# The opening stage of a decoder trunk: the conditioning vector spread by the matrix engine, low parts of two weights formed there, loads in another order, later work queued behind the stage

## The chip, the cores and the metric

The kernel runs on one core of one Trainium2 chip. The metric is the device time of one execution in microseconds (us). Engines are named as in the profile: PE is TensorE's matmul, PEld its weight load, DVE is VectorE, ACT is ScalarE, POOL is GpSimd, and SP is SyncE, whose queue (SPq) issues nearly all DMAs. The five run side by side, each in the order of its own instruction stream, and wait for each other on semaphores.

## The reference, cut to what matters

One layer of a decoder, sequence 2048, width 1024, float32, batch 1.

```python
c_act = jax.nn.silu(c)                                   # (1, 1024)
mod = (c_act @ w_ada[l] + b_ada[l])[:, None, :]          # 6 * 1024 conditioning values
sh1, sc1, g1, sh2, sc2, g2 = jnp.split(mod, 6, axis=-1)
h = rms_norm(x) * (1.0 + sc1) + sh1
x = x + g1 * token_mixer(h, w_in[l], ...)                # one in-projection, 11 head groups, one out-projection
h = rms_norm(x) * (1.0 + sc2) + sh2
x = x + g2 * conv_ffn(h, w_up[l], ...)
return rms_norm(x) * final_gain
```

Nothing of the in-projection can begin before the norm of the first 512 rows of `x` is known and, for each 128 columns of `h`, the two conditioning values `sc1` and `sh1` of those columns.

## The kernel before

**Tiling.** The 2048 rows are four blocks of 512 (`TB`); the width of 1024 is eight tiles of 128 (`KD`), so a block of `x` is eight tiles x[0] to x[7] of 128 partitions by 512. A product in float32 is made of three products of a rounded type (`F32R`): each operand is split into a high part (a cast) and a low part (the value minus the cast), and `split3` multiplies high by high, high by low and low by high. The high part is an ACT cast; the low part is a DVE subtraction of a 128x1024 tile.

**The opening, `startup()`.** For the first block it does by hand what later blocks find done: eight loads of x[k]; squares on ACT (`sumsq`, L336 and L339) that DVE adds up (L340, tile `san`); a PE product with a column of ones (`ssn`, L412); an inverse square root by Newton steps on DVE (L153 to L158, tile `rsn`); a PE product that spreads it to 512 columns (`bcn`, L420) and an ACT copy of that (`bc`, L423). Then eight steps k. In step k DVE makes x[k] = x[k] * sc1 * bc (`scaled`, L346), ACT makes the high part of `h` (`high`, L350, tile `ha`), DVE its low part (`low`, L353), and PE multiplies the tile by three weight pieces of the first HGRN2 unit: `f` and `q` (L434, into the PSUM tiles `pshfh` and `pshqh`) and `v` (L440, into `psvgh`; `v0` holds the rows of steps 0 to 3, `v1` those of 4 to 7).

**The conditioning.** Each of the 48 groups of 128 values is one DVE instruction over a 128x1024 tile of `w_ada` (`cond` or `ada`, L197, tile `wada`; shown as CUSTOM_DVE_ANT_0 with a short reading of the sum behind it), which multiplies by `c_act`, the activated vector repeated on all 128 partitions. Group 8+k is `sc1` of step k, group k is `sh1`. Sixteen of them lie in the opening. `c_act` is made from `craw`, a load that reads the 4 KB vector once for each partition (L176, 512 KB), a sigmoid on ACT (L177) and a product on DVE (L178).

**Loads.** SP issues them in order. The weights of the opening go into `wraw`, a ring of two buffers (`NRAW`), so the raw piece of `v0` (`rv`) can only be loaded once the low part of `f` has read its buffer. A ring of eight tiles (`a4k`) holds `c_act`, `craw`, the `wada` tiles and the two parts of `v1`.

**What sets the order.** PE's order is written out by hand for the whole kernel (`tc.manual_schedule(engines={PE})`). Inside `startup()` that of DVE, ACT and SP is too. Behind it a scheduler orders DVE, ACT and SP by priority and readiness, and it may place instructions of later code between those of the opening: `gla_weights` (L713 to L719, the small weight `alow`, its DVE row is L717), the weights of the second unit (`rakg`, `raqg`, split at L229 and L233 into `hakg`, `lakg`, `haqg`, `laqg`). The low parts of the weights are stored for later blocks (`keep`, L208).

After the opening PE goes on with `alg` (L728), `psakg`, level products of the first unit (`lvh`, L610) and `psaqg`, without another stage of this kind; the MLP behind it is a long run of `split3` products.

Of the kernel before, what the change touches and what calls it, by code (L numbers as in the profile page):

```python
# [9 lines left out]
F32 = mybir.dt.float32  # L10
# [7 lines left out]
P = 128  # L18
D = 1024
# [81 lines left out]
def trunk(ctx, tc, xT, vecs, cvec, cst, rope, msk, wada, win, walow, wgla, wout, wup, wdown, out):  # L101
# [70 lines left out]


    c_act = pa.tile([P, D], F32, tag="a4k", name="c_act")
    craw = pa.tile([P, D], F32, tag="a4k", name="craw")
    nc.sync.dma_start(craw[:], cvec.to_broadcast([P, D]))  # L176
# [157 lines left out]
    def sumsq(acc, x, k, name, sl=slice(0, TB), first=None, room=None):  # L334
        if k == 0 if first is None else first:
            S.activation(acc[:, sl], x[:, sl], AF.Square)  # L336
        else:
            sq = (room or late)(f"sq{name}{k}")
            S.activation(sq[:, sl], x[:, sl], AF.Square)  # L339
            V.tensor_tensor(acc[:, sl], acc[:, sl], sq[:, sl], op=ALU.add)  # L340
# [4 lines left out]
    def scaled(t, bc, k):  # L345
        V.scalar_tensor_tensor(t, t, SC1[:, k:k + 1], bc, op0=ALU.mult, op1=ALU.mult)  # L346
# [5 lines left out]
    def low(t, k):  # L352
        V.scalar_tensor_tensor(h[k][:, 1, :], t, SH1[:, k:k + 1], h[k][:, 0, :], op0=ALU.add, op1=ALU.subtract)  # L353
# [13 lines left out]
    def new_bc1(b):  # L367
        return px.tile([P, TB], F32, tag="bc1", name=f"bc1_{b}", bufs=1)

    def startup():  # L370
# [5 lines left out]
            nc.sync.dma_start(x[k], xT[0, :, k, :])  # L376
        raws = {}

        def weight(name, i, extra=False):
            raw = pw.tile([P, 1024], F32, tag="wraw", name="r" + name, bufs=NRAW)  # L380
            nc.sync.dma_start(raw[:], win[i])
            if extra:
                t = [pa.tile([P, 1024], F32R, tag="a4k", name=n + name) for n in "hl"]
            else:
                t = [pw.tile([P, 1024], F32R, tag="w" + n, name=n[0] + name) for n in ("hi", "lo")]
            W[name] = [*t, raw, i]

        def cast(name):
            S.copy(W[name][0][:], W[name][2][:])

        def low_part(name):
            hi, lo, raw, i = W[name]
            V.tensor_tensor(lo[:], raw[:], hi[:], op=ALU.subtract)

        def cond(m):
# [18 lines left out]
        V.tensor_scalar(ms[:], ps[:, 0:NCH], 1.0 / D, EPS, op0=ALU.mult, op1=ALU.add)  # L414
        newton(ms, r, NCH)
        cast("f")
        bc = bc1[0] = new_bc1(0)
        ps = late_ps("bcn1_0")
        for c in range(NCH):
            T.matmul(ps[:, c * P:(c + 1) * P], r[:, c:c + 1].to_broadcast([P, P]), ident, start=True, stop=True)  # L420
        cond(0)
        cond(9)
        S.copy(bc[:], ps[:])  # L423
        cast("q")
# [19 lines left out]
        def flush():  # L444
            for q in list(pending):
# [1 line left out]
                    pending.remove(q)  # L447
                    put(*q)

        plan = [((10,), (), (1,), "f"), ((3, 11), (), (2,), "q"), ((4,), (10,), (3,), "v0"),  # L450
                ((12, 5), (11,), (4,), None), ((13, 6), (12,), (5,), "v1"), ((14, 7), (13,), (6,), None),
                ((15,), (14,), (7,), None), ((), (15,), (), None)]
        parts = {"f", "q"}, set()
        for k, (ld, first, then, wl) in enumerate(plan):
            if k == 0:
                weight("v0", 2)
            if k == 3:
                weight("v1", 3, True)
            load(*ld)
            for m in first:  # L460
                cond(m)
            scaled(x[k], bc[:], k)
            high(x[k], k, "0_")
            if k in (1, 4):
                name = "v0" if k == 1 else "v1"
                cast(name)
                parts[0].add(name)
            for m in then:
                cond(m)
            low(x[k], k)  # L470
# [242 lines left out]
    def gla_weights():  # L713
        raw = pt.tile([P, KD, 16], F32, tag="te", name="alraw", bufs=NTE)
        nc.sync.dma_start(raw[:], walow)
        S.copy(alow[:, :, 0:16], raw[:])
        V.tensor_tensor(alow[:, :, 16:32], raw[:], alow[:, :, 0:16], op=ALU.subtract)  # L717
        nc.sync.dma_start(gup[0:16, :], wgla)
        nc.sync.dma_start(gup[16:32, :], wgla)  # L719

    def unit_g(b, pos):
        nm = f"g{b}"
# [315 lines left out]
    jobs = [job for k in range(NF // 2) for job in (("d", k), ("u", 2 * k + 1 if k < 10 else 0))]  # L1038
    for b in range(NB):
        pos = 0  # L1040
        if b == 2:
            later += range(40, 48)
        for i, (kind, u) in enumerate(ORDER):
# [521 lines left out]
```

## Time and profile before

| what | us |
|---|---|
| median of 3 runs | 2544.25 |
| the runs | 2546.16, 2537.70, 2544.25 |
| the profiled execution | 2538.74 |
| its span, first to last instruction | 2537.0 |
| PE busy in the span | 2478.0 (98%) |
| PE busy in the first 59.0 us | 31.97 |
| PE busy from 59.0 to 120.0 us | 61.00 |

Rows of the timeline read: start, length, engine, line, operation, output <- inputs, shape, count, and in brackets how long the engine had been idle and whose end released it. Rows with x above 1 are several instructions in one line. Two DVE instructions that follow each other overlap by about 0.1 us, so the distance of two starts is a little less than a row's length. A list of DMAs gives, for each kind, its size and the median time from issue to landing.

### The profile page before, as it was taken

How to read it: one execution, taken by the hardware profiler on the slowest of the kernel's cores; microseconds unless marked ns; L12 is line 12 of the kernel's file. 1: busy time of each engine (PE TensorE's matmuls, PEld its weight loads, DVE VectorE, ACT ScalarE, POOL GpSimd, SP SyncE). 2: the span in 40 equal slices, each digit the busy share in tenths (PEclk: the TensorE clock that was granted, in tenths of full speed). 3: DMA queues.
4: the chain of work that ended last, by engine and by line, in shares of the span. 5: the costliest groups of instructions: out<-in, count | busy, mean ns of one | idle time of the engine just before them, and what ended most of it. 6: DMA issues, size and time to landing. Idle time of an engine off the chain costs nothing.

```text
span 2537.0 us, 36995 instructions
## 1 busy us (share of the span) xinstructions
PE 2478.0 (98%) x13146; PEld 2106.8 (83%) x13146; DVE 1949.7 (77%) x3568; ACT 1134.1 (45%) x1906; POOL 151.4 (6%) x271
## 2 busy tenths in 40 slices
PE   5999999999999999999999999999999999999998
PEld 4889888888889888898788888888878888888887
DVE  8788985878678676767688888887678777778666
ACT  4433434423443235333455555455445545545442
POOL 1000000000000000000100000000001010010000
PEclk9999999999999999999999999999999999999999
DMA  8454576675687846884754444487665544447653
GB/s 304 163 198 166 197 259 226 223 272 196 221 325 250 286 161 230 294 301 152 236 184 150 161 156 144 145 291 251 203 223 186 159 137 152 151 133 265 215 191 125
DMA packets 228057, 525.45 MB, mean 207 GB/s; under 512 B 24960, under 2 KB 28064, under 8 KB 227872
## 3 DMA queue, kind: packets, MB, share of 16 engines
q1 hardware_dynamic: 224672, 512.60, 59.3%
q0 software_dynamic: 3200, 10.49, 1.2%
q8 instruction: 103, 1.69, 0.3%
q14 instruction: 82, 0.67, 0.1%
HBM read 393.49 MB, written 129.50 MB: 206 GB/s over the span
## 4 chain that ended last, share of the span: by engine, by line
PE 59%; DMA 4%; DVE 4%; issue 1%; ACT 1%; SPq 0%; DVEq 0%; ACTq 0%; POOLq 0%
PE X L241 6%; PE X L242 6%; PE X L243 6%; PE Z L242 3%; PE Z L243 3%; PE Z L241 3%; PE dX L241 3%; PE dX L242 3%; PE dX L243 3%; PE lvh L610 2%; PE Y L242 2%; PE Y L243 2%; PE Y L241 2%; PE psqkvgr L243 1%; PE psqkvgr L241 1%
## 5 line engine op out<-in xcount | busy, mean ns | idle before, releaser
L241 PE MATMUL X<-B,A 128*128 128x512 f32 x572 | 223.1, 390 | 1.4 <-ACT u L1246 1.4
L243 PE MATMUL X<-B,A 128*128 128x512 f32 x572 | 222.6, 389 | 0.0
L242 PE MATMUL X<-B,A 128*128 128x512 f32 x572 | 222.5, 389 | 0.0
L973 DVE TENSOR_TENSOR dA<-rd,dA 128x512 fp32r<-128x512 f32 x154 | 106.3, 691 | 91.2 <-ACT dA L972 90.5
L972 ACT CAST dA<-rd 128x512 fp32r<-128x512 f32 x154 | 95.5, 620 | 148.9 <-PE dX L243 59.6
L242 PE MATMUL dX<-dB,dA 128*128 128x512 f32 x396 | 154.3, 390 | 2.2 <-DVE dB L973 2.2
L241 PE MATMUL dX<-dB,dA 128*128 128x512 f32 x396 | 154.2, 389 | 1.6 <-DVE y L1424 1.6
L243 PE MATMUL dX<-dB,dA 128*128 128x512 f32 x396 | 154.1, 389 | 0.0
L973 DVE TENSOR_TENSOR A<-s,A 128x512 fp32r<-128x512 f32 x176 | 120.8, 687 | 40.5 <-ACT A L972 40.3
L241 PE MATMUL psvgh<-hvgh,ha 128*128 128x256 f32 x480 | 140.9, 293 | 0.0
L243 PE MATMUL psvgh<-hvgh,ha 128*128 128x256 f32 x480 | 136.3, 284 | 0.0
L242 PE MATMUL psvgh<-lvgh,ha 128*128 128x256 f32 x480 | 136.2, 284 | 0.0
L972 ACT CAST A<-s 128x512 fp32r<-128x512 f32 x176 | 108.6, 617 | 56.3 <-PE Z L243 43.5
L241 PEld LDWEIGHTS X<-B,A 128*128 128x128 f32 x572 | 107.5, 188 | 24.4 <-ACT u L1246 2.2
L243 PEld LDWEIGHTS X<-B,A 128*128 128x128 f32 x572 | 107.4, 188 | 22.3
L242 PEld LDWEIGHTS X<-B,A 128*128 128x128 f32 x572 | 107.4, 188 | 22.2
L242 PE MATMUL Z<-B,A 128*128 128x512 f32 x308 | 120.7, 392 | 4.3 <-DVE B L973 4.3
L610 PE MATMUL lvh<-qbh,kh 128*128 128x128 f32 x896 | 120.3, 276 | 1.4 <-DVE nw L157 1.3
L610 PEld LDWEIGHTS lvh<-qbh,kh 128*128 128x128 f32 x896 | 114.7, 190 | 7.8 <-issue 1.8
L241 PE MATMUL Z<-B,A 128*128 128x512 f32 x308 | 120.7, 392 | 0.5 <-ACT B L972 0.5
L243 PE MATMUL Z<-B,A 128*128 128x512 f32 x308 | 120.3, 391 | 0.0
L973 DVE TENSOR_TENSOR dB<-rb,dB 128x512 fp32r<-128x512 f32 x154 | 105.6, 687 | 8.4 <-ACT dB L972 8.3
(458 smaller groups left out, 6981.6 us busy)
## 6 DMA issues: line engine op xcount, KB each, us to landing
gs<-yv SPq DMA_DIRECT2D x154, 256.0 KB, 2.9
rb<-gs SPq DMA_DIRECT2D x154, 256.0 KB, 4.0
r<-wup SPq DMA_DIRECT2D x141, 256.0 KB, 3.3
s<-sumsu SPq DMA_DIRECT2D x132, 256.0 KB, 3.0
wada<-wada SPq DMA_DIRECT2D x48, 512.0 KB, 4.9
rd<-sumsd SPq DMA_DIRECT2D x88, 256.0 KB, 4.0
rd<-wdown SPq DMA_DIRECT2D x66, 256.0 KB, 3.5
x<-xT SPq DMA_DIRECT2D x64, 256.0 KB, 5.7
```

The source lines that it names most:

```text
L241: T.matmul(ps, lhs[0], rhs[0], start=first, stop=False, skip_group_check=more)
L242: T.matmul(ps, lhs[0], rhs[1], start=False, stop=False, skip_group_check=more)
L243: T.matmul(ps, lhs[1], rhs[0], start=False, stop=last, skip_group_check=more)
L610: T.matmul(ps[:, c * P:(c + 1) * P].rearrange("p (h n s) -> p h n s", h=2, s=s), kq[rs, c * P:(c + 1) * P], rhs, start=True, stop=True)
L972: S.copy(hi, src)
L973: V.tensor_tensor(lo, src, hi, op=ALU.subtract)
```

## The change

- `c_act`: the vector is loaded as eight rows of 128 (`c_row`, 4 KB); PE transposes it to a column (`ct`), ACT and DVE activate the 128x8 column (`csig`, `ccol`), eight PE products of 128 columns in float32 spread it over the partitions (`cb`), and ACT copies the two PSUM banks to `c_act`.
- Low parts of `f` and `q`: for each half of 512 columns PE multiplies the raw weight by the identity (float32) and the cast by minus the identity (`minus`, F32R) into one bank, and ACT copies it out (`low_sum`, `low_out`). Those of `v0` and `v1` stay on DVE.
- Loads: `v0` and `v1` get raw buffers of their own (tag `qbd`); the weights and the `wada` tiles of the first steps are issued in another order; the small loads (`alraw`, `gup`, `m_all`) come behind the last `wada` tile.
- `plan`: the conditioning groups of step k+1 are made in step k as before, the order of 2 and 10 is turned; the low part of `v0` comes in step 1 (before: step 2).
- The squares use six buffers in place of two (`room=tmp`).
- `issue_after`: in block 0, everything traced behind `startup()` and `gla_weights()` stands behind three named instructions on SP, ACT and DVE.

```diff
-    craw = pa.tile([P, D], F32, tag="a4k", name="craw")
-    nc.sync.dma_start(craw[:], cvec.to_broadcast([P, D]))
-    S.activation(c_act[:], craw[:], AF.Sigmoid)
-    V.tensor_tensor(c_act[:], c_act[:], craw[:], op=ALU.mult)
+    c_row = pt.tile([KD, P], F32, tag="te", name="c_row", bufs=NTE)
+    nc.sync.dma_start(c_row[:], cvec.rearrange("o (k p) -> (o k) p", p=P))
...
+            if name in "fq":
+                raw = pw.tile([P, 1024], F32, tag="wraw", name="r" + name, bufs=NRAW)
+            else:
+                raw = p1.tile([P, 1024], F32, tag="qbd", name="r" + name, bufs=3)
...
+        def low_sum(name, j):
+            hi, lo, raw, i = W[name]
+            sl = slice(j * 512, (j + 1) * 512)
+            ps = halves[name, j] = lev_ps(f"low{name}{j}")
+            T.matmul(ps[:], ident, raw[:, sl], start=True, stop=False)
+            T.matmul(ps[:], minus[:], hi[:, sl], start=False, stop=True)
+
+        def low_out(name, j):
+            S.copy(W[name][1][:, j * 512:(j + 1) * 512], halves.pop((name, j))[:])
...
-        load(8, 0)
+        load(8)
         weight("f", 1)
-        load(9)
+        load(0)
         weight("q", 0)
-        load(1, 2)
+        load(9, 1)
+        weight("v0", 2)
+        load(10)
+        pc_ = late_ps("ct")
+        T.transpose(pc_[:, 0:KD], c_row[:], ident[0:KD, 0:KD])
+        cs, cc = small("csig", KD), small("ccol", KD)
+        S.activation(cs[:], pc_[:, 0:KD], AF.Sigmoid)
+        V.tensor_tensor(cc[:], pc_[:, 0:KD], cs[:], op=ALU.mult)
+        cb = [lev_ps(f"cb{j}") for j in range(2)]
+        for k in range(KD):
+            T.matmul(cb[k // 4][:, (k % 4) * P:(k % 4 + 1) * P], cc[:, k:k + 1].to_broadcast([P, P]), ident, start=True, stop=True)
...
-            sumsq(acc, x[k], k, "n1_0_")
+            sumsq(acc, x[k], k, "n1_0_", room=tmp)
+        for j in range(2):
+            S.copy(c_act[:, j * 512:(j + 1) * 512], cb[j][:])
+        S.mul(minus[:], ident, -1.0)
         cond(8)
...
-        plan = [((10,), (), (1,), "f"), ((3, 11), (), (2,), "q"), ((4,), (10,), (3,), "v0"),
...
+        plan = [((2,), (1,), (), None, ()), ((11,), (10,), (2,), "v0", ("v0",)), ((3,), (11,), (3,), None, ()),
...
+            scaled(x[k], bc[:], k)
+            high(x[k], k, "0_")
             if k == 0:
-                weight("v0", 2)
...
+                low_sum("f", 1)
+                low_out("f", 1)
+                for j in range(2):
+                    low_sum("q", j)
+                    low_out("q", j)
...
-    nc.sync.dma_start(m_all[:], msk[:, 0:320])
-    gla_weights()
+        last = gla_weights()
+        first = [nc.sync.dma_start(m_all[:], msk[:, 0:320]).ins, *last]
...
+    behind = ExitStack()
+    for ins in first:
+        behind.enter_context(tc.issue_after(ins))
```

Three places of the instruction streams show what moves. The first is DVE's stream in steps 0 and 1 (`x` is `scaled`, `ha` the low part of `h`, ISA the conditioning). Before:

```order
L346 SCALAR_TENSOR_TENSOR x_0_345<-x_0_345,mod,bc_0_419 128x512
L197 ISA wada_371,mod<-wada_371,c_act,vec 128x1024
L197 ISA mod 128x1
L353 SCALAR_TENSOR_TENSOR ha_0_440<-x_0_345,mod,ha_0_440 128x512
L393 TENSOR_TENSOR lf<-rf,hf 128x1024
L346 SCALAR_TENSOR_TENSOR x_0_345<-x_0_345,mod,bc_0_419 128x512
L197 ISA wada_373,mod<-wada_373,c_act,vec 128x1024
L197 ISA mod 128x1
L353 SCALAR_TENSOR_TENSOR ha_1_455<-x_0_345,mod,ha_1_455 128x512
L393 TENSOR_TENSOR lq<-rq,hq 128x1024
L717 TENSOR_TENSOR alow<-alraw,alow 128x8x16
```

The same place of the changed kernel's DVE stream, up to the first row of step 2:

```order
L344 SCALAR_TENSOR_TENSOR x_0_343<-x_0_343,mod,bc_0_444 128x512
L195 ISA wada_369,mod<-wada_369,c_act,vec 128x1024
L195 ISA mod 128x1
L351 SCALAR_TENSOR_TENSOR ha_0_462<-x_0_343,mod,ha_0_462 128x512
L344 SCALAR_TENSOR_TENSOR x_0_343<-x_0_343,mod,bc_0_444 128x512
L195 ISA wada_375,mod<-wada_375,c_act,vec 128x1024
L195 ISA mod 128x1
L351 SCALAR_TENSOR_TENSOR ha_1_491<-x_0_343,mod,ha_1_491 128x512
L195 ISA wada_459,mod<-wada_459,c_act,vec 128x1024
L195 ISA mod 128x1
L394 TENSOR_TENSOR lv_374<-rv_371,hv_373 128x1024
L344 SCALAR_TENSOR_TENSOR x_2_346<-x_2_346,mod,bc_0_444 128x512
```

The rows of `lf`, `lq` and `alow` are gone from here, and that of `lv` for `v0` stands one step earlier.

The second is PE's stream at its beginning, in the changed kernel. Before, the four `ssn` and the four `bcn` products were all that stood ahead of the first `pshfh`.

```order
L422 MATMUL ct<-c_all,c_row 128x8
L428 MATMUL cb_383<-c_all,ccol 128x128 x4
L428 MATMUL cb_384<-c_all,ccol 128x128 x4
L439 MATMUL ssn_0_421<-c_all,san_0_394 128x1 x4
L402 MATMUL lowf_441<-rf,c_all 128x512
L403 MATMUL lowf_441<-hf,minus 128x512
L448 MATMUL bcn_0_445<-c_all,rsn_0_427 128x128 x4
L402 MATMUL lowf_464<-rf,c_all 128x512
L403 MATMUL lowf_464<-hf,minus 128x512
L402 MATMUL lowq_468<-rq,c_all 128x512
L403 MATMUL lowq_468<-hq,minus 128x512
L402 MATMUL lowq_472<-rq,c_all 128x512
```

One half of `f` stands ahead of `bcn`, the other three halves behind it.

The third is SP's queue at the end of the opening. Before, the load of `raqg` stood ahead of the store of `lakg`:

```order
L208 DMA kepti1l<-lf 128x1024
L208 DMA kepti0l<-lq 128x1024
L208 DMA kepti2l<-lv_436 128x1024
L208 DMA kepti3l<-lv_522 128x1024
L228 DMA raqg_784<-win 128x1024
L208 DMA kepti17l<-lakg_732 128x1024
```

In the changed kernel:

```order
L226 DMA rakg_765<-win 128x1024
L206 DMA kepti1l<-lf 128x1024
L206 DMA kepti0l<-lq 128x1024
L206 DMA kepti2l<-lv_374 128x1024
L206 DMA kepti3l<-lv_489 128x1024
L206 DMA kepti17l<-lakg_764 128x1024
L226 DMA raqg_816<-win 128x1024
```

`raqg` now stands behind a store that waits for DVE's low part of the piece before it. From the instructions on that the trace of before shows at about 80 us, the streams of all engines hold the same instructions in the same order in both kernels.

More of the change, by code (lines that the diff above doesn't have):

```diff
@@ L416, in startup @@
         cast("f")
+        low_sum("f", 0)
         bc = bc1[0] = new_bc1(0)
@@ L448, in flush @@
                     put(*q)
-        plan = [((10,), (), (1,), "f"), ((3, 11), (), (2,), "q"), ((4,), (10,), (3,), "v0"),
[L451 to L454, printed above, removed]
-            if k == 0:
-                weight("v0", 2)
-            if k == 3:
-                weight("v1", 3, True)
-            load(*ld)
+        plan = [((2,), (1,), (), None, ()), ((11,), (10,), (2,), "v0", ("v0",)), ((3,), (11,), (3,), None, ()),
+                ((12, 4), (12,), (4,), "v1", ("v1",)), ((13, 5), (13,), (5,), None, ()), ((14, 6), (14,), (6,), None, ()),
+                ((15, 7), (15,), (7,), None, ()), ((), (), (), None, ())]
+        parts = {"f", "q"}, {"f"}
+        for k, (ld, first, then, wl, wc) in enumerate(plan):
+            load(*ld)
+            if k == 1:
+                weight("v1", 3)
+            scaled(x[k], bc[:], k)
+            high(x[k], k, "0_")
+            if k == 0:
+                low_sum("f", 1)
[3 more added lines that the diff above has]
+                    low_out("q", j)
+                parts[1].add("q")
+            for name in wc:
+                cast(name)
+                parts[0].add(name)
             for m in first:
                 cond(m)
[L462 to L467, printed above, removed]
+            low(x[k], k)
             for m in then:
                 cond(m)
-            low(x[k], k)
             if wl:
```

19 lines of the change are left out of this document (12 added, 7 removed).

## The prediction

> **What bounds the kernel now.** First the page and the busy time by stages: PE is the bound, and the opening is the only long stretch where it is not.
>
> ```profile
> span 2537.0 us, 36995 instructions
> PE 2478.0 (98%) x13146; PEld 2106.8 (83%) x13146; DVE 1949.7 (77%) x3568; ACT 1134.1 (45%) x1906; POOL 151.4 (6%) x271
> ...
> 0.00:59.00 59.00, 31.97 (x161) 26.25 (x161) 47.05 (x81) 22.44 (x31) 11.26 (x22) 1.00 0.82 304
> 59.00:120.00 61.00, 61.00 (x338) 49.81 (x339) 43.03 (x94) 30.01 (x56) 1.99 (x3) 1.00 0.52 181
> ```
>
> PE idles 59.0 us in all and 27.0 of them before 59.0 us; in the 61 us behind that it is never idle. So what the opening ends earlier should carry to the end, and nothing else in the kernel changes. The marks of the opening are in PE's and ACT's timelines:
>
> ```profile
> 14.48 1.87 PE L412 MATMUL ssn<-c_all,san 128*128 128x1 f32 x8 [14.48 <-DVE san L340]
> 18.58 2.07 PE L420 MATMUL bcn<-c_all,rsn 128*128 128x128 f32 x8 [2.23 <-DVE rsn L158]
> 30.00 2.08 PE L440 MATMUL psvgh<-hv,ha 128*128 128x256 f32 x8 [3.94 <-ACT hv L389]
> 34.00 1.20 PE L440 MATMUL psvgh<-hv,ha 128*128 128x256 f32 x8
> 55.66 0.50 PE L434 MATMUL pshfh<-ha,hf 128*128 128x512 f32 x1 [0.54 <-DVE ha L353]
> 58.99 0.42 PE L728 MATMUL alg<-ha,alow 128*32 128x512 f32 x1 [0.48 <-ACT snh L691]
> 7.64 0.63 ACT L336 ACTIVATE san<-x 128x512 f32<-128x512 f32 x1 [0.33 <-DMA x<-xT]
> 8.30 2.03 ACT L339 ACTIVATE sqn<-x 128x512 f32<-128x512 f32 x3
> 20.69 0.59 ACT L423 COPY bc<-bcn 128x512 f32<-128x512 f32 x1 [3.52 <-PE bcn L420]
> 16.12 1.04 ACT L389 CAST hf<-rf 128x1024 fp32r<-128x1024 f32 x1 [2.62 <-DMA rf<-win]
> 28.90 1.04 ACT L389 CAST hv<-rv 128x1024 fp32r<-128x1024 f32 x1 [2.42 <-DMA rv<-win]
> 53.85 0.73 ACT L350 ACTIVATE ha<-x,mod 128x512 fp32r<-128x512 f32 x1 [3.14 <-DVE x L346]
> ```
>
> The opening ends at 58.99, where `alg` begins, 3.33 us after the last low part of `h` lets PE go (55.66). That low part is DVE's, so I read DVE's timeline back from there:
>
> ```profile
> 8.96 5.47 DVE L340 TENSOR_TENSOR san<-san,sqn 128x512 f32<-128x512 f32 x7 [0.40 <-ACT sqn L339]
> 21.31 0.75 DVE L346 SCALAR_TENSOR_TENSOR x<-x,mod,bc 128x512 f32<-128x512 f32 x1 [0.37 <-ACT bc L423]
> 23.85 1.22 DVE L393 TENSOR_TENSOR lf<-rf,hf 128x1024 fp32r<-128x1024 f32 x1
> 24.98 0.74 DVE L346 SCALAR_TENSOR_TENSOR x<-x,mod,bc 128x512 f32<-128x512 f32 x1
> 27.51 1.22 DVE L393 TENSOR_TENSOR lq<-rq,hq 128x1024 fp32r<-128x1024 f32 x1
> 28.64 0.28 DVE L717 TENSOR_TENSOR alow<-alraw,alow 128x128 fp32r<-128x128 f32 x1
> 30.16 1.28 DVE L197 CUSTOM_DVE_ANT_0 wada<-wada,c_act,vec 128x1024 f32<-128x1024 f32 x1 [1.23 <-DMA wada<-wada]
> 45.34 0.75 DVE L346 SCALAR_TENSOR_TENSOR x<-x,mod,bc 128x512 f32<-128x512 f32 x1
> 49.20 0.75 DVE L346 SCALAR_TENSOR_TENSOR x<-x,mod,bc 128x512 f32<-128x512 f32 x1
> 53.06 0.75 DVE L346 SCALAR_TENSOR_TENSOR x<-x,mod,bc 128x512 f32<-128x512 f32 x1
> 53.73 1.22 DVE L233 TENSOR_TENSOR lakg<-rakg,hakg 128x1024 fp32r<-128x1024 f32 x1
> 54.86 0.75 DVE L353 SCALAR_TENSOR_TENSOR ha<-x,mod,ha 128x512 fp32r<-128x512 f32 x1
> ```
>
> From 21.31 to 55.61 DVE has one idle row, the 1.23 us for a `wada` load. A step costs 3.86 us (45.34, 49.20, 53.06): a scaling, a low part, two conditionings. PE needs less and waits. So the opening is a front up to 21.31, set by loads and the chain through `san`, `ssn`, `rsn` and `bc`, and then a DVE stretch.
>
> **The change, part by part: the DVE stretch.** The thirteen conditionings, eight scalings and eight low parts of `h` all stay. What leaves:
> - `lf` and `lq`: each takes 1.13 us from its start to the next start (23.85 to 24.98, 27.51 to 28.64). Together -2.26.
> - `alow` and the wait behind it: 28.64 to 30.16, -1.52. The wait goes because SP no longer holds `wada` group 10 behind `rv`, which stood in the queue until `lf` freed a `wraw` buffer; now `rv` has its own.
> - `lakg`: in its place DVE waits for ACT's last high part. From the scaling's start to ACT's start is 0.79, ACT takes 0.73, a hand-over 0.04: 1.56 us, against 1.80 (53.06 to 54.86). -0.24.
> - `lv` for both halves of `v` stays on DVE, one merely a step earlier: 0.
>
> Sum of the stretch: -4.02.
>
> **The front.** DVE's seven adds run without a gap in 5.47 us, 0.78 each, from the end of the second square on. Six buffers for the squares instead of two therefore give nothing; the cover is that DVE chain itself. What counts is when x[1] lands, 8.30 (its square begins ACT's second row). Rows for that:
>
> ```profile
> 1.67 0.42 SPq L176 DMA_DIRECT2D craw<-cvec  x1
> 2.13 4.44 SPq L376 DMA_DIRECT2D x<-xT  x8
> ...
> x<-xT SPq DMA_DIRECT2D x10, 256.0 KB, 5.9
> craw<-cvec SPq DMA_DIRECT2D x1, 512.0 KB, 4.6
> c_all<-cst SPq DMA_DIRECT2D x1, 136.5 KB, 2.6
> ...
> gs<-yv SPq DMA_DIRECT2D x154, 256.0 KB, 2.9
> ```
>
> The 512 KB of `craw` stand just ahead of the eight tiles and become 4 KB. At the rate behind it (tiles of 256 KB landed about 0.65 us apart: the three squares of ACT's second row take 2.03) its bytes alone are worth 1.3 us, so x[1] at 7.0: that end excludes less. The other end: x[1] is issued at about 2.6, and 256 KB with nothing in the way land in 2.9 us, so at 5.5. Between them I take 5.5, since the only large transfer ahead is then x[0] itself, which is nearer to the free transfer than to the queue of before. x[1] comes 2.8 us earlier (bounds 1.3 and 2.8), the last add ends at 11.6, and the chain `ssn`, Newton, `bcn`, `bc` keeps its length of 6.88 us (14.43 to 21.31): -2.8.
>
> What the front adds: the transpose, 8x128 sigmoid and product need `c_row` and the identity in `c_all`, both issued ahead of the x tiles; `c_all` lands 2.6 us after an issue before 1.67, so they are over near 5 us. The eight `cb` products are two `bcn` rows, 4.1 us, on a PE that had no work until 14.48. Two copies to `c_act` (0.59 each, as `bc`) and `minus` follow the last square on ACT, end near 12 and stand ahead only of `hf`, whose raw weight came at 16.12 and now has 1 MB less ahead of it (`craw` and one `wada`), so it comes at 12 to 13 by the same rate. Nothing there is on the path. The later `wada` tiles come one per 1.3 us at that rate, and DVE takes two in 3.86, so none is late. The first half of `f` is made while Newton runs (about 2 us, `bcn` before it started at 14.43 + 4.15).
>
> **The three other halves.** They stand behind `bcn` on PE, and their copies stand on ACT ahead of the second high part, for which DVE waits. A half is 512 columns in float32 and 512 rounded:
>
> ```profile
> 76.51 1.12 PE L739 MATMUL zg<-alg,gup 32*128 32x512 f32 x2
> 24.57 1.05 PE L434 MATMUL pshqh<-ha,hq 128*128 128x512 f32 x2
> ```
>
> At full rate 1.1 us (the `zg` row is one such float32 product with its latency), at the slow rate of the opening 2.1 (the `bcn` row has the same 512 columns; a rounded one costs 0.43). The two `psvgh` rows show the rate: eight products took 2.08 at 30.00 and 1.20 at 34.00, so PE runs at half rate until about 4 us of unbroken work. In the changed kernel unbroken work starts with the first half of `f` at 13.6, so full rate from 17.6, just as `bcn` ends (17.9). The halves end at 19.0, 20.1 and 21.8 (the last needs a bank that is copied out behind ACT's first high part), the copy at 22.4, the second high part at 23.2, and DVE, which would come to the low part at 18.53 + 4.41 = 22.94 (18.53 is where the first scaling now starts; two scalings, a low part, two conditionings), waits 0.3. The bounds: 0, and at the slow rate throughout 2.9. I take +0.3.
>
> The Trainium skill, "TensorE: Matmul & The Clock Gate", Part 1, says that the full rate comes after one busy window of about 3.4 us, that the windows run freely, and that one idle window takes it away. The two `psvgh` rows agree with the first part. By that rule the start at 13.6 could be answered as late as 20.4, an estimate from its two windows, and the sum would be about 0.7 us smaller.
>
> **The sum.** -4.02 - 2.8 + 0.3 = -6.5 us: `alg` at 52.5 in place of 58.99. The profiled execution took 2538.74 (span 2537.0 and 1.7 around it), so 2532.2; it lies 5.5 below the median of the three runs, 2544.25, and the same 6.5 off the median gives the forecast, 2537.7. PE's added work, some 4.1 + 4 halves, is paid out of its 27 idle us.
>
> Later work is cast later: `hakg` and `lakg`, then `raqg`. `lakg` follows the last low part and ends near 51, well before `psakg` would read it (16 `alg` products behind 52.5). `raqg` is the third rival below. The held-back POOL clears of `qbd` buffers now wait for `v0` and `v1`; the first that meets a waiter is used after `psaqg`, 30 us later.
>
> **Rivals.**
> 1. The front moves only by the bytes of `craw` (1.3): the sum is -5.0, 2539.2. For it: the DMA engines are 0.82 busy over the opening, by the row quoted first. Against it: the latency of a free tile.
> 2. PE stays at half rate through the three halves, so DVE waits 2.9: -3.9, 2540.3. For it: PE idles from the `cb` products to `ssn`. Against: the 4 us between the `psvgh` rows.
> 3. Slower than before: `raqg` is late. Its load now waits on SP behind the store of `lakg`, so it is issued near 51.3 (before, at 46.30).
>
> ```profile
> raqg<-win SPq DMA_DIRECT2D x1, 512.0 KB, 6.9
> ...
> 50.00:55.00 5.00, 4.38 (x25) 3.38 (x23) 4.96 (x8) 1.44 (x2) 0.18 (x1) 1.00 0.45 149
> ...
> 69.89 0.48 PE L241 MATMUL psaqg<-ha,haqg 128*128 128x512 f32 x1
> ```
>
>  With 6.9 us to land it is there at 58.2, cast at 59.3 and split at 60.5; `psaqg` wants it at 69.89 - 6.5 = 63.4. So 2.9 us are spare. PE then stops one for one, and the kernel is slower than before only from 9.4 us more on; at 20 us to land it would cost 10.2, 2548. Against it: the DMA engines were 0.45 busy there.
> 4. The gain is taken back later by a wait that does not move: 2544. Against it: 61.00 of 61.00 us busy, and the same order of instructions behind 80 us.
> 5. More than forecast: `bcn` at full rate takes 0.3 off the chain, no wait for the halves another 0.3: -7.1, 2537.1.
>
> **How the numbers follow.** A measurement of this kernel tells about 0.3%, 7.6 us, from no change; the three runs alone spread over 8.5. The forecast has 0.58, rivals 1 and 2 together 0.18, rival 3 0.04, rival 4 0.06, rival 5 0.14. The forecast's 6.5 is 1.1 short of 7.6, so with that spread I count half of its chance, 0.29, as faster by over 0.3%, with 0.10 of rival 5 and 0.06 of 1 and 2: 0.45. Slower by over 0.3% is rival 3, 0.04. The rest, 0.51, is within. The range: from the largest sum, 2537.1, down by the 6.6 that the lowest run lies below its median, so 2530.5; upward to rival 4, 2544.0.
>
> **What would show it.** `ssn` at 11.6 in place of 14.48; the first scaling at 18.5; no `lf`, `lq`, `alow` or DMA wait in DVE's rows before the last low part; the row of step 2's scaling near 26.4; `alg` at 52.5; PE fully busy from there. Wrong, if x[1] lands at 7, if the second high part waits on the halves for microseconds, or if `psaqg` waits for `haqg`.

## The result, and the profile after

Twenty runs of each kernel: the changed kernel took 2535.94 us in the median (2531.37 to 2542.38), the kernel before 2543.12 us (2537.7 to 2549.39). The ratio is 0.9973, with a 95% interval of 0.9965 to 0.9982. That is 7.2 us or 0.28% less, which by the 0.3% of the prediction counts as no change, though the interval excludes a ratio of 1. A later comparison (11 runs against 20, in the last experiment below) gave 0.9973 again, with 0.9961 to 0.9985; its medians lie 5.4 us apart.

The profiled execution took 2537.37 us. Its page and the busy time by stages, in the columns of the prediction's first fence:

```profile
span 2535.6 us, 37063 instructions
PE 2489.7 (98%) x13175; PEld 2114.7 (83%) x13175; DVE 1949.3 (77%) x3566; ACT 1136.8 (45%) x1913; POOL 152.1 (6%) x271
...
0.00:52.00 52.00, 37.87 (x184) 30.45 (x185) 42.67 (x77) 22.55 (x34) 11.21 (x22) 0.90 0.83 302
...
59.00:120.00 61.00, 60.67 (x350) 50.49 (x349) 44.84 (x90) 28.85 (x51) 1.99 (x3) 1.00 0.52 186
```

PE idles 45.9 us now in place of 59.0; its busy time grew by 11.7 us, so the spans of this one pair differ by only 1.4 us, although the opening ends 5.4 us earlier. The rest of the execution scatters by more than that (last column of the table below). The marks of the opening, from PE's and ACT's timelines of the changed kernel:

```profile
13.73 1.87 PE L439 MATMUL ssn<-c_all,san 128*128 128x1 f32 x8 [4.17 <-DVE san L338]
15.46 2.05 PE L402 MATMUL lowf<-rf,c_all 128*128 128x512 f32 x2
...
19.57 1.02 PE L402 MATMUL lowf<-rf,c_all 128*128 128x512 f32 x2
53.55 0.42 PE L762 MATMUL alg<-ha,alow 128*32 128x512 f32 x1 [0.48 <-ACT snh L724]
...
5.66 0.63 ACT L334 ACTIVATE san<-x 128x512 f32<-128x512 f32 x1 [1.24 <-DMA x<-xT]
6.30 0.63 ACT L337 ACTIVATE sqn<-x 128x512 f32<-128x512 f32 x1
8.34 3.23 ACT L337 ACTIVATE sqn<-x 128x512 f32<-128x512 f32 x5 [1.41 <-DMA x<-xT]
12.32 0.63 ACT L337 ACTIVATE sqn<-x 128x512 f32<-128x512 f32 x1 [0.76 <-DMA x<-xT]
```

And DVE's timeline, which the opening follows as before:

```profile
9.00 4.67 DVE L338 TENSOR_TENSOR san<-san,sqn 128x512 f32<-128x512 f32 x6 [1.35 <-ACT sqn L337]
20.39 0.75 DVE L344 SCALAR_TENSOR_TENSOR x<-x,mod,bc 128x512 f32<-128x512 f32 x1 [0.20 <-ACT bc L453]
25.06 0.75 DVE L351 SCALAR_TENSOR_TENSOR ha<-x,mod,ha 128x512 fp32r<-128x512 f32 x1 [0.19 <-ACT ha L348]
40.42 0.74 DVE L344 SCALAR_TENSOR_TENSOR x<-x,mod,bc 128x512 f32<-128x512 f32 x1
44.16 0.74 DVE L344 SCALAR_TENSOR_TENSOR x<-x,mod,bc 128x512 f32<-128x512 f32 x1
47.89 0.74 DVE L344 SCALAR_TENSOR_TENSOR x<-x,mod,bc 128x512 f32<-128x512 f32 x1
49.43 0.75 DVE L351 SCALAR_TENSOR_TENSOR ha<-x,mod,ha 128x512 fp32r<-128x512 f32 x1 [0.79 <-ACT ha L348]
```

Three numbers sum up the opening, and the experiments use them: the **front** (start of the first scaling, 20.39; before 21.31), the **stretch** (from there to the start of the last low part of `h`, 49.43 - 20.39 = 29.04; before 54.86 - 21.31 = 33.55), and **`alg`** (53.55; before 58.99). From the last low part to `alg` it is 4.12, as before (4.13).

### The profile page after: what moved, and what is told of

Same layout as the page of the kernel before. It is cut to its first block, busy times and chain, and to the rows that moved or that the text cites. A ratio compares the mean times of both kernels' runs of the same rounds, so it can differ in the third digit from the quotient of the medians.

```text
span 2535.6 us, 37063 instructions
## 1 busy us (share of the span) xinstructions
PE 2489.7 (98%) x13175; PEld 2114.7 (83%) x13175; DVE 1949.3 (77%) x3566; ACT 1136.8 (45%) x1913; POOL 152.1 (6%) x271
## 4 chain that ended last, share of the span: by engine, by line
PE 58%; DVE 5%; DMA 4%; issue 1%; ACT 1%; SPq 0%; DVEq 0%; ACTq 0%; POOLq 0%
PE X L239 6%; PE X L240 6%; PE X L241 6%; PE Z L240 3%; PE dX L239 3%; PE Z L241 3%; PE dX L240 3%; PE dX L241 3%; PE Z L239 3%; PE Y L239 2%; PE Y L240 2%; PE Y L241 2%; PE dY L239 1%; PE dY L241 1%; PE dY L240 1%
```

## The experiments

Each kernel below is the changed kernel with one edit, one run with a profile, unless said otherwise. All of them in one table; "one time" is that of the profiled execution, and "the rest" is that time less `alg`.

| kernel | front | stretch | `alg` | one time | the rest |
|---|---|---|---|---|---|
| before (two executions) | 21.31, 21.93 | 33.55, 33.38 | 58.99, 59.44 | 2538.74, 2543.81 | 2479.8, 2484.4 |
| changed (three) | 20.39, 19.95, 19.83 | 29.04, 29.05, 29.04 | 53.55, 53.13, 53.01 | 2537.37, 2538.77, 2541.73 | 2483.8, 2485.6, 2488.7 |
| weight loads held back | 20.36 | 29.03 | 53.53 | 2542.12 | 2488.6 |
| x tiles in two groups | 21.71 | 29.04 | 54.88 | 2547.58 | 2492.7 |
| conditioning vector as before | 21.10 | 29.06 | 54.29 | 2533.31 | 2479.0 |
| `f`, `q` low parts on DVE | 19.61 | 31.05 | 54.79 | 2543.91 | 2489.1 |
| later work not held back | 20.12 | 32.37 | 56.87 | 2540.17 | 2483.3 |
| conditionings in the old order | 20.57 | 30.04 | 54.75 | 2545.31 | 2490.6 |
| `v` low parts on POOL | 19.68 | 31.20 | 55.01 | 2544.42 | 2489.4 |
| `v1` low part on PE | 19.88 | 28.52 | 52.54 | 2538.04 | 2485.5 |
| both `v` low parts on PE | 20.91 | 27.37 | 52.42 | 2539.67 | 2487.2 |

The last column is why an experiment is judged by its marks and not by its one time: behind the opening all kernels run the same work, and yet it varies from 2479 to 2493. It goes with the clock that TensorE was granted in the mean of the execution: the four with 0.994 or more (both of before, the conditioning vector as before, later work not held back) have 2479.0 to 2484.4, the ten others, with 0.990 to 0.992, have 2483.8 to 2492.7. The rests of before, 2482.1 in the mean, lie below those of the three changed executions, 2486.0; that nothing of the gain is given back behind the opening therefore rests on the medians and ratios alone. In the later comparison the mean granted clock was the same for both kernels (0.9934 and 0.9935). The fronts of kernels whose front was not edited vary from 19.68 to 20.91 (eight executions, mean 20.17); the stretches of the changed kernel agree within 0.01.

**Both kernels once more.** No edit.

> The kernel before, unchanged, for a second profile. If the opening repeats from execution to execution and the scatter of the runs lies behind it, alg begins at 58.99 within 0.3 us and the stretch from there to the end differs from the first profile's 2478.0 us by microseconds. If the opening itself scatters, alg moves by microseconds too.

> The changed kernel, unchanged, for a second profile. Opening repeats: alg at 53.55 within 0.3 us, x[7]'s square near 12.3, the reciprocal on DVE again 2.3 us long if that belongs to the kernel and 0.2 if it was chance; the stretch behind alg between 2476 and 2483 us. Opening scatters: alg anywhere between 52 and 55.

The table's first two lines have the marks. `alg` repeats within 0.45 us before and 0.54 us after, not within the expected 0.3, and the rest of the second changed execution, 2485.6, lies above the expected 2483. Most of the scatter of `alg` lies in the front; the stretch repeats. The long reciprocal (2.31 us in the first execution) was 0.18 in the second and 2.23 in the third, without a later front where it was long. The means of `alg` are 59.22 before and, with the third execution, 53.23 after: 6.0 us earlier, by 1.56 in the front (21.62 to 20.06) and 4.4 in the stretch. The 7.2 us of the medians agrees with that: the interval of the ratio is 4.6 to 8.9 us of 2543.

**The front: loads behind the x tiles held back.** A tiny load out of the fifth x tile stands ahead of the first conditioning load on SP, so nothing of the weights is in flight until that tile has landed.

```diff
+        gate = pdr.tile([1, 16], F32, tag="gate", name="gate")
+        nc.sync.dma_start(gate[:], x[4][0:1, 0:16])
         load(8)
```

> The changed kernel with one added DMA of 64 bytes out of x[4] ahead of the first conditioning load, so that SP holds that load and the first weight until x[4] has landed. Theory (the loads queued behind x[0..7] now start earlier and share the DMA engines with them, so x[7] lands no earlier than before): x[7]'s square starts at 10.9 or earlier in place of 12.32, the last add ends at 12.6 or earlier in place of 13.67, alg at 52.6 or earlier in place of 53.55. Rival (the DMA engines deliver at a lower rate in the first 10 us whatever is queued): x[7]'s square stays within 0.4 us of 12.32 and alg does not come earlier than 53.3.

ACT's and DVE's timelines of this run:

```profile
8.00 3.96 ACT L337 ACTIVATE sqn<-x 128x512 f32<-128x512 f32 x6 [1.23 <-DMA x<-xT]
...
8.66 4.67 DVE L338 TENSOR_TENSOR san<-san,sqn 128x512 f32<-128x512 f32 x6 [1.17 <-ACT sqn L337]
```

All tiles had landed in time for squares without a gap, where the changed kernel's last square waited until 12.32. But x[2] still came only at 8.0, and the six adds behind it, 0.78 each, end at 13.33 against 13.67, 13.28 and 12.95 in the three executions of the changed kernel. The theory fell: holding the loads behind back brought the last tiles earlier, not the one that starts the chain. Of the rival's marks `alg` came (53.53), the late last square did not.

**The front: x tiles in two groups.** The same tiny load out of x[0], ahead of x[3].

```diff
+            if k == 3:
+                gate = pdr.tile([1, 16], F32, tag="gate", name="gate")
+                nc.sync.dma_start(gate[:], x[0][0:1, 0:16])
             nc.sync.dma_start(x[k], xT[0, :, k, :])
```

> The changed kernel with a tiny load that reads the first tile of x put ahead of the loads of the fourth to eighth tile, so that only three of them are in flight at first. Theory (the tiles in flight share the DMA engines, so that a tile lands late because seven others go beside it): x[2]'s square begins at 7.0 us or earlier, the seven adds end at 12.3 or earlier, the first scaling is at 19.2 or earlier, `alg` at 52.5 or earlier. Rival (the rate in the first 8 us is low whatever is in flight): x[2]'s square begins at 7.8 or later, the adds end at 13 or later, the first scaling is at 20 or later and `alg` at 53.1 or later.

ACT's and DVE's timelines of this run, and one of its windows (the last columns are the granted clock, the DMA engines' busy share and GB/s):

```profile
6.03 1.26 ACT L337 ACTIVATE sqn<-x 128x512 f32<-128x512 f32 x2
8.62 2.13 ACT L337 ACTIVATE sqn<-x 128x512 f32<-128x512 f32 x3 [1.32 <-DMA x<-xT]
12.67 1.31 ACT L337 ACTIVATE sqn<-x 128x512 f32<-128x512 f32 x2 [1.93 <-DMA x<-xT]
...
13.33 1.49 DVE L338 TENSOR_TENSOR san<-san,sqn 128x512 f32<-128x512 f32 x2 [1.77 <-ACT sqn L337]
```

```profile
6.00:8.00 2.00, 2.00 (x11) 2.00 (x11) 1.20 (x2) 1.26 (x2) 0.00 (x0) 1.00 0.64 194
```

With three tiles in flight x[2]'s square follows x[1]'s at once, at about 6.7 in place of 8.34, 7.22 and 7.62 in the three executions of the changed kernel: tiles in flight do share the engines, as the theory had it. Its other numbers fell, since the wait for the group left the engines at 0.64 from 6 to 8 us and the last two tiles came only at 12.67, with the adds' end at 14.82. The rival's later marks came true, for another reason than it gave. So either way some tile comes late. That the rate of the first microseconds sets the front is argued from this, not shown by a run of its own. That rate, by windows of the changed kernel:

```profile
6.00:8.00 2.00, 1.99 (x9) 1.99 (x10) 0.69 (x1) 0.92 (x2) 0.00 (x0) 1.00 0.92 274
8.00:10.00 2.00, 1.56 (x9) 1.36 (x8) 0.89 (x2) 1.64 (x3) 0.00 (x0) 1.00 1.02 320
14.00:16.00 2.00, 2.00 (x9) 1.94 (x10) 1.57 (x4) 1.17 (x2) 0.00 (x0) 0.50 1.04 424
```

**The conditioning vector as before.** 512 KB spread by the load, sigmoid and product over the whole tile; the transpose, the `cb` products and their copies are gone, all else is the changed kernel's.

```diff
+    craw = pa.tile([P, D], F32, tag="a4k", name="craw")
+    nc.sync.dma_start(craw[:], cvec.to_broadcast([P, D]))
...
-            T.matmul(cb[k // 4][:, (k % 4) * P:(k % 4 + 1) * P], cc[:, k:k + 1].to_broadcast([P, P]), ident, start=True, stop=True)
```

> The changed kernel with the conditioning vector made as before: 512 KB load, sigmoid on ACT, product on DVE; no transpose and no spreading on PE. Theory (that part bought only some 0.8 us, since its bytes were given to the loads behind): first scaling near 21.3 in place of 20.39, alg at 54.3 to 54.8. Rival (the vector's load was worth its full 2.8 us and something else in the changed kernel took 2 us back): alg at 55.5 or later.

```profile
8.75 5.47 DVE L340 TENSOR_TENSOR san<-san,sqn 128x512 f32<-128x512 f32 x7 [0.28 <-ACT sqn L339]
21.10 0.75 DVE L346 SCALAR_TENSOR_TENSOR x<-x,mod,bc 128x512 f32<-128x512 f32 x1 [0.38 <-ACT bc L445]
```

DVE's timeline of that run: the adds run without a gap again and end at 14.22, and the front is 21.10, against 20.39, 19.95 and 19.83, as the theory had it. By these three this part is worth 0.7 to 1.3 us. It is one execution, though, and against all eight fronts that were not edited (19.68 to 20.91) it is 0.2 to 1.4, 0.9 in the mean: at most about the 1.3 of its bytes, and not 2.8.

**The stretch: low parts of `f` and `q` on DVE.**

```diff
-            if k == 0:
-                low_sum("f", 1)
...
+            if k < 2:
+                low_part("fq"[k])
+                parts[1].add("fq"[k])
```

> The changed kernel with the low parts of f and q made by DVE again, in steps 0 and 1, and no low sums on PE; all else as changed. DVE's stretch from the first scaling to the start of the last low part was 29.04, 29.05, 29.03 and 29.06 us in four profiles of the changed kernel and its variants (33.55 and 33.38 before). Theory (DVE is the bound, each of the two costs its 1.14 us there, and the wait of 0.2 for the second high part goes): 31.1 us, alg at 55.4. Rival (the stretch has slack for them, the gain came from loads and order): 29.1 to 29.5, alg at 53.4 to 53.9.

The stretch is 31.05 in place of 29.04, +2.0, where the two DVE instructions alone are 2.26. Most of the difference is the 0.19 that DVE otherwise waits for a high part behind the halves' copies (row at 25.06 above). The term is as predicted. `alg` came at 54.79 and not at the 55.4 expected, because the front of this execution was early (19.61).

**The stretch: later work not held back.** The weights of `alg` and what follows are left to the scheduler again, which may place them in the opening.

```diff
-        last = gla_weights()
...
-    for ins in first:
-        behind.enter_context(tc.issue_after(ins))
```

> The changed kernel without the held-back later work: the mask load and the small weights behind startup() outside its hand-written order, no issue_after. DVE's stream then has alow and lakg in step 4, and SP's has stores and raqg ahead of the last six conditioning loads. Theory (each DVE row in the stretch costs its length): stretch 29.05 + 0.25 + 1.14 = 30.4 us, alg at 54.8; nothing behind alg is gained. Rival (the conditioning loads are late behind those DMAs): a DMA wait in DVE's rows of step 4 or 5 and a stretch over 31. Second rival (holding back bought nothing): 29.1.

ACT's timeline of this run, and DVE's:

```profile
30.69 0.30 ACT L749 CAST alow<-alraw 128x128 fp32r<-128x128 f32 x1 [5.00 <-DMA alraw<-walow]
30.90 0.72 ACT L348 ACTIVATE ha<-x,mod 128x512 fp32r<-128x512 f32 x1
...
31.65 0.75 DVE L351 SCALAR_TENSOR_TENSOR ha<-x,mod,ha 128x512 fp32r<-128x512 f32 x1 [1.90 <-ACT ha L348]
39.06 0.28 DVE L750 TENSOR_TENSOR alow<-alraw,alow 128x128 fp32r<-128x128 f32 x1
39.26 1.22 DVE L231 TENSOR_TENSOR lakg<-rakg,hakg 128x1024 fp32r<-128x1024 f32 x1
```

The stretch is 3.33 longer; the theory had 1.4. Its two instructions are there (0.20 and 1.14 on DVE). The other 1.90 is a wait: ACT sat 5.00 us at the cast of `alow`, whose load was late, with the high part of step 2 behind it, and DVE waited for that. The rival had the stretch right and its cause wrong: DVE waits for no conditioning load. Holding work back is thus worth most by keeping a cast of something late out of an in-order queue ahead of something urgent. Of the parts that were undone alone it is the largest.

**The stretch: conditionings in the old order.** Loads and casts stay; a scaling again follows directly on the conditioning whose result it reads.

```diff
-                ((12, 4), (12,), (4,), "v1", ("v1",)), ((13, 5), (13,), (5,), None, ()), ((14, 6), (14,), (6,), None, ()),
+                ((12, 4), (11,), (4,), "v1", ("v1",)), ((13, 5), (12,), (5,), None, ()), ((14, 6), (13,), (6,), None, ()),
...
+            for m in first:
+                cond(m)
             scaled(x[k], bc[:], k)
```

> The changed kernel with the conditionings in the order of before: group 8+k directly ahead of step k's scaling, which reads it, and group k+1 between scaling and low part. Same instructions, other order. Theory (a scaling directly behind the conditioning it reads waits 0.12 us for the sum, six times): stretch 29.05 + 0.7 = 29.8 us, steps 3.86 us apart in place of 3.74, alg at 54.1. Rival (the 0.12 us has another cause, for instance the DMA traffic or the store of lakg): steps stay at 3.74 and the stretch at 29.1.

```profile
41.23 0.08 DVE L195 DVE_READ_ACCUMULATOR2_ANT mod<- 128x1 f32 x1
41.35 0.75 DVE L344 SCALAR_TENSOR_TENSOR x<-x,mod,bc 128x512 f32<-128x512 f32 x1
...
43.23 0.08 DVE L195 DVE_READ_ACCUMULATOR2_ANT mod<- 128x1 f32 x1
43.23 0.74 DVE L351 SCALAR_TENSOR_TENSOR ha<-x,mod,ha 128x512 fp32r<-128x512 f32 x1
...
45.21 0.75 DVE L344 SCALAR_TENSOR_TENSOR x<-x,mod,bc 128x512 f32<-128x512 f32 x1
```

DVE's timeline of this run: a step is 3.86 again (41.35, 45.21), against 3.74 in the changed kernel (40.42, 44.16, 47.89). The rows show where: the scaling starts 0.12 behind the short reading of the sum that it needs (41.23, 41.35); the low part, which needs an older sum, starts at the same moment as the reading ahead of it (43.23). The same four instructions cost 0.12 more when the scaling reads what the instruction just ahead of it wrote. Six steps have it: 0.72 of the 1.0 us that the stretch grew; 0.18 more is a wait for the cast of `v0`, which the old order meets earlier. The list of the change says that step k made the groups of step k+1 before as well; from step 2 on, the kernel before made group 8+k in step k itself, directly ahead of the scaling that reads it.

**Next: low parts of `v` on POOL.** A trial to go further, with POOL idle for most of the stretch.

```diff
-            V.tensor_tensor(lo[:], raw[:], hi[:], op=ALU.subtract)
+            G.tensor_tensor(lo[:], raw[:], hi[:], op=ALU.subtract)
```

> The changed kernel with the two remaining low parts, those of v0 and v1, made by POOL in place of DVE. Theory (DVE is the bound of the opening): stretch 29.05 - 2 * 1.14 = 26.8 us, alg at 51.1 to 51.5, where PE begins to be the bound. Rival (POOL's 128x1024 subtraction takes several us or slows DVE beside it, and PE waits for the low parts in step 1 and 4): PE idle ahead of psvgh with lv grows from 1.0 to over 3 us, alg at 53 or later.

The timelines of POOL, DVE and PE:

```profile
25.60 3.11 POOL L394 TENSOR_TENSOR lv<-rv,hv 128x1024 fp32r<-128x1024 f32 x1 [19.73 <-ACT hv L390]
...
25.23 1.28 DVE L195 CUSTOM_DVE_ANT_0 wada<-wada,c_act,vec 128x1024 f32<-128x1024 f32 x1
...
26.43 2.82 DVE L344 SCALAR_TENSOR_TENSOR x<-x,mod,bc 128x512 f32<-128x512 f32 x1
...
28.77 1.23 PE L469 MATMUL psvgh<-lv,ha 128*128 128x256 f32 x4 [2.04 <-POOL lv L394]
```

The scaling that runs beside POOL's subtraction takes 2.82 in place of 0.74 (and 2.88 beside the second one, which takes 3.50). The stretch becomes 31.20, not 26.8: taking two instructions of 1.13 off DVE made its stretch 2.2 us longer. The rival's slower DVE came true, its wait of over 3 us on PE did not (2.04). The Trainium skill, "GPSIMD Engine Reference", section 1, Specifications, says that POOL's way to the on-chip memory is shared with VectorE and names contention with DVE instructions that have two inputs there. This run agrees for the scaling, with 2.82 against 0.74. It doesn't for every instruction with two inputs: a conditioning reads two tiles too, and the one that starts at 25.23, beside POOL's first 0.9 us, keeps its 1.28, as does one beside the second subtraction (1.27 from 34.79, POOL from 34.82). What tells the two apart no run here shows, and the lengths of POOL's rows are rough.

**Next: low parts of `v` on PE.** First that of `v1` alone, both halves at once; then both, one half at a time, each ahead of the step that reads it. The second kernel was timed in ten runs, beside eleven of the changed kernel.

```diff
-                ((12, 4), (12,), (4,), "v1", ("v1",)), ((13, 5), (13,), (5,), None, ()), ((14, 6), (14,), (6,), None, ()),
+                ((12, 4), (12,), (4,), None, ("v1",)), ((13, 5), (13,), (5,), None, ()), ((14, 6), (14,), (6,), None, ()),
...
+                if name == "v1":
+                    for j in range(2):
+                        low_sum(name, j)
+                        low_out(name, j)
```

> The changed kernel with the low part of `v1` formed by PE as those of `f` and `q` are (two halves, copied out by ACT); that of `v0` stays on DVE. Theory (DVE is the bound of the stretch to its end, and PE and ACT have room in it): the stretch from the first scaling to the start of the last low part of `h` is 27.9 us in place of 29.05, and `alg` comes at 52.0 to 52.4. Rival (PE or ACT is full by then): PE's four more products and ACT's two more copies push the high parts or the products back, the stretch is 28.7 us or more, or `alg` comes more than 3.6 us after the last low part, and is at 53 or later.

```diff
...
+            if k in (2, 5):
+                low_sum(f"v{k // 4}", 1)
+                low_out(f"v{k // 4}", 1)
...
+            if k in (1, 4):
+                low_sum(f"v{k // 4}", 0)
+                low_out(f"v{k // 4}", 0)
...
```

> The changed kernel with the low parts of both halves of `v` formed by PE, one half of the columns at a time, each just ahead of the step whose products read it, so that a copy does not stand ahead of a high part on ACT. Theory (DVE is the bound; the half step that the run with `v1` alone lost was ACT's copy of a second half ahead of a high part): the stretch is 26.8 us (29.05 less 2 x 1.13), `alg` at 51.3 or earlier, and the median is 1.8 to 2.3 us below that of the changed kernel beside it, 0.996 of the kernel before. Rival (PE and its rate are the bound once two more halves of each part stand in its stream): the stretch is 28 us or more, `alg` at 52.5 or later, the median is that of the changed kernel within 1 us.

> The changed kernel once more, timed on the same chip in the same rounds, for comparison. By the two profiles so far `alg` comes at 53.1 to 53.6, 5.4 to 6.3 us ahead of the kernel before; if the time follows `alg` alone, the median is 5.9 us below that of the kernel before, 0.9977. If something behind the opening adds to it, as the 7.2 us between the two medians would have it, it is 7 us or more below, 0.9972 or less.

Each low part on PE takes 1.13 us from DVE, but in either run a wait of 0.5 us, once, gave part of that back. DVE's row of the first, then PE's, ACT's and DVE's rows of the second:

```profile
37.51 0.75 DVE L351 SCALAR_TENSOR_TENSOR ha<-x,mod,ha 128x512 fp32r<-128x512 f32 x1 [0.52 <-ACT ha L348]
```

```profile
31.13 1.02 PE L402 MATMUL lowv<-rv,c_all 128*128 128x512 f32 x2
...
32.41 0.59 ACT L406 CAST lv<-lowv 128x512 fp32r<-128x512 f32 x1 [3.45 <-PE lowv L403]
32.89 0.73 ACT L348 ACTIVATE ha<-x,mod 128x512 fp32r<-128x512 f32 x1
...
33.65 0.75 DVE L351 SCALAR_TENSOR_TENSOR ha<-x,mod,ha 128x512 fp32r<-128x512 f32 x1 [0.51 <-ACT ha L348]
```

The half stands in PE's stream behind the products of the step before, so it is made at 31.13; its copy stands in ACT's stream ahead of the high part of step 3, whose scaling was started at 31.19 and could have been read from 31.98 on. Hence 0.5 us, and a stretch of 27.37, between the theory's 26.8 and the rival's 28; the run with `v1` alone had 28.52, between 27.9 and 28.7. `alg` at 52.42 has a late front in it (20.91). The median was 2537.39 us (2534.2 to 2540.6), ratio to before 0.9970 (0.996 to 0.998). The changed kernel beside it had 2539.10 (2534.26 to 2541.73), ratio 0.9973 (0.9961 to 0.9985). The 1.7 us between them are what the stretch says (29.04 less 27.37), but the intervals overlap almost wholly: that this version beats the changed kernel is not shown by its times. Nor does the comparison decide what was expected of the changed kernel beside it: its median lies 5.4 us below that of the kernel before (2544.49), nearer to `alg` alone, its ratio of 0.9973 nearer to the other.

## Why the prediction was right, and by which steps

The forecast, 2537.7 in a range of 2530.5 to 2544.0, with "same" likelier than "faster", met a measured 2535.9 and 0.28%. `alg` came 6.0 us earlier where 6.5 were forecast. Two terms were mis-sized in opposite directions, and that they cancel to half a microsecond is luck. So is, in part, a time that lies within 1.8 us of the forecast, which was counted from the median of three runs that scatter by 8.5 us:

- **The front, -2.8: it was -1.56** (means of two and three executions). The step that failed is "What counts is when x[1] lands", with 5.5 for it. The square of x[1] began at 6.30, two of the 2.8 us earlier, but DVE then stood 1.35 us for x[2] (row at 9.00), and the chain of adds started anew from there (in the second execution it did so for x[3], after 0.82); `ssn` began at 13.73, where 11.6 was forecast. The reading behind the step was wrong too: the square of x[1] follows that of x[0] without a wait in both kernels (7.64 and 8.30 before, 5.66 and 6.30 now), so 8.30 does not show the landing of x[1] but the end of the square of x[0], and the 0.65 us for a tile was ACT's own pace over three squares that waited for nothing. Between a free tile and a tile behind others I had chosen the free one, since only x[0] stood ahead; the run with two groups shows that tiles issued later share the engines with those ahead of them too. Rival 1, that only the bytes of `craw` count (1.3), had the size of this term right.
- **The reorder of the conditionings, 0: it was -0.72.** The prediction counted the instructions of a step and found the same four. It had the row spacing of 3.86 and did not ask whether the order of the four was part of it. The old order costs 0.12 a step, in six steps.
- `lf` and `lq`, -2.26, `alow` with the wait behind it, -1.52, and `lakg`, -0.24: the stretch fell by 4.4 in the mean, which is these 4.02, the 0.72 and a loss of 0.19 (DVE's wait at 25.06) and some 0.1 besides. The first is confirmed by its own run. The second and third together cost 3.33 when undone alone, because in the new order of loads the wait falls on another load, `alraw`, at another place; that says what the hold is worth in this kernel, not that the term was wrong.
- The three other halves, +0.3: measured 0.19, so that rival 2, with 2.9, fell. From the first scaling to the second low part it is 25.06 - 20.39 = 4.67, where 4.41 + 0.3 were put.
- The six buffers for the squares, nothing: adds that follow each other still take 0.78 each (4.67 for six).
- Rival 3: `raqg` was issued at 54.14, 2.8 us later than supposed, and split at 59.88; `psaqg` began at 64.45, with no wait. The store ahead of it was late because `lakg` came at 52.47 and not right behind the last low part; the profile names no engine or load for that wait of 2.08 (`issue`), and its cause stays open. These timelines show it:

```profile
52.47 1.23 DVE L231 TENSOR_TENSOR lakg<-rakg,hakg 128x1024 fp32r<-128x1024 f32 x1 [2.08 <-issue]
...
54.14 0.38 SPq L226 DMA_DIRECT2D raqg<-win  x1
...
59.88 1.23 DVE L231 TENSOR_TENSOR laqg<-raqg,haqg 128x1024 fp32r<-128x1024 f32 x1 [1.61 <-ACT haqg L227]
...
64.45 0.48 PE L239 MATMUL psaqg<-ha,haqg 128*128 128x512 f32 x1
```

- Rival 4, a gain given back: two comparisons with a ratio of 0.9973 each exclude it.
- PE's rate: half until about 19.4, not 17.6. The window rows have the granted clock in the third column from the end:

```profile
18.00:19.00 1.00, 1.00 (x5) 1.00 (x6) 1.00 (x3) 0.93 (x2) 0.00 (x0) 0.50 1.03 410
19.00:20.00 1.00, 1.00 (x7) 0.76 (x6) 1.00 (x1) 0.23 (x1) 0.00 (x0) 0.79 1.03 410
```

That is 5.7 us after `ssn` began, where I took 4 from the `psvgh` rows; the 20.4 that the prediction worked out by the Trainium skill, "TensorE: Matmul & The Clock Gate", Part 1, as the latest time holds. It cost nothing only by luck, since the front came 1.9 us later than forecast, and the second half of `f`, at 19.57, already ran at 1.02. The column does not show every slow stretch: in the trace of before it reads 1.00 all through the opening, although eight `psvgh` products took 2.08 at 30.00 and 1.20 at 34.00.

What stays open: how much of the front's 1.56 us is the conditioning vector's (21.62 less 21.10 leaves 0.5 for the rest, from one execution, where fronts scatter by 1.2); and whether the 0.9 us between `alg` (6.0) and the ratio (6.9) is anything but scatter, with 2479 to 2493 us behind `alg`.

## What to carry to other kernels

Where one engine runs a written-out order without idling, compare where each row starts with the start of the row ahead of it: an instruction that reads the small result of the one just ahead cost 0.12 us here that no row shows as idle, and putting one other instruction between them gave it back. An off-path load can still set the pace when its cast stands in an in-order queue ahead of urgent work, so look at what each engine's queue holds behind a late load. And work moved to an idle engine pays only if that engine's own stream has a free place for it at the right moment, and if it doesn't slow the engine that it relieves, as POOL did.

## What was not expected of the hardware

- A DVE instruction that reads the accumulated result of the one just ahead of it comes 0.12 us later than with another in between (3.86 against 3.74 a step), with no idle time shown.
- POOL's two-input subtraction slows the scaling on DVE beside it from 0.74 to 2.82 us, and not a conditioning beside it (1.28).
- From 6 to 10 us the DMA engines moved 274 to 320 GB/s at a busy share of 0.92 and more; at 14 us it was 424.
- PE fell to half rate for 3.4 us in the middle of the stretch, after some 2.5 us with PE about half busy, in two of the three profiled executions of the same kernel; the third had idle gaps much like them and kept full rate. The windows of the one and of the other:

```profile
38.00:39.00 1.00, 0.50 (x1) 0.19 (x1) 1.00 (x3) 0.18 (x1) 0.00 (x0) 1.00 0.47 188
40.00:41.00 1.00, 1.00 (x6) 0.90 (x5) 1.00 (x3) 0.00 (x0) 0.39 (x1) 0.50 0.97 381
```

```profile
38.00:39.00 1.00, 0.38 (x2) 0.21 (x2) 1.00 (x4) 0.00 (x0) 0.00 (x0) 1.00 0.41 168
40.00:41.00 1.00, 1.00 (x9) 0.94 (x8) 1.00 (x2) 0.36 (x1) 0.94 (x1) 1.00 0.91 306
```

In windows of 0.1 us the granted clock changes at 12.59, 19.41, 39.89 and 43.31 in the one and at 12.97 and 19.80 in the other, always 3.41 us or a multiple of it apart. In the 3.41 us ahead of the drop PE was busy for 1.91 us, in both executions that fell; in the third, on its own grid (36.87 to 40.28), for 1.98. So it seems that the busy share of such a fixed stretch counts, and where it lies against the gaps; that is worked out from these three executions and not tested further. The drop cost nothing here, since DVE sets the pace there: its steps stay at 3.74.
